# The front of a hybrid decoder block: every engine's order written out by hand instead of planned by priorities

## The chip, the cores and the metric

The kernel runs on one core of one Trainium2 chip. A core has TensorE (matrix products into PSUM), VectorE, ScalarE and GpSimd (called DVE, ACT and POOL in the profile) and SyncE, whose queue (SP) issues the DMA transfers here. Every engine works through its own queue in order and waits on semaphores for the others. The metric is device time in microseconds for one execution.

## What is computed

A decoder block over 512 positions of 1024 channels: a mixer of two halves (an S5 state space model and a chunked gating unit), then a PEER expert layer, then a gated embedding. The change concerns what stands ahead of PEER:

```python
xn = _rmsnorm(h, ln_mix_g[i])
z = xn @ w_in[i]
xs, u, v = z[..., :D_SSM], z[..., D_SSM:D_SSM + D_SGU], z[..., D_SSM + D_SGU:]
ys = _gelu(_s5(xs, ...))                               # diagonal complex recurrence + d * u
ys = ys * jax.nn.sigmoid(ys @ glu_w[i] + glu_b[i])
yg = _sgu(u, v, ...)                                   # gelu(u) * (tril(W_s) LN(gelu(v)) + b)
mix = jnp.concatenate([_rmsnorm(ys, out_norm_ssm[i]), _rmsnorm(yg, out_norm_sgu[i])], axis=-1)
h = h + mix @ w_out[i]
hn = _rmsnorm(h, ln_ffn_g[i])                          # PEER starts here
```

## The kernel before

Positions lie in four tiles of 128 (`NT`), channels in blocks of 128. The front goes through these stages, by the lines of `before.py`:

- x is loaded and transposed (L264), scaled into `xn` (L267, ScalarE), and multiplied with the first 512 columns of `w_in` in full f32 (`pz`, L278). ScalarE copies the product out by position modulo four into `u4` (L289), and VectorE scales it (L291).
- The embedding's projection `pj` (L304) has nothing to do with the rest; it is stored to memory (`pjd`) for the end of the kernel.
- VectorE works out the S5 parameters from 16-column tiles (L310 to L434): two exponentials, an angle, powers of the transition, squarings (`csquare`). From these come tables `rc`, `rs` of a complex exponential over 128 columns, doubled seven times (the `tab` loop under L557).
- The recurrence runs in four groups g of four pairs. `s5_r` makes operands on VectorE, `s5_par` (L481 to L498) transposes them on TensorE and copies them out on ScalarE, with a kernel matrix `ptt` whose third product adds the skip term d through an identity (L487); `s5_pv` (L506) makes the inputs of the scan, `s5_scan` (L518 to L526) scans on VectorE, `s5_back` rotates back, `s5_q` makes the output operands, `s5_out` (L543 to L548) multiplies them, and ScalarE applies sixteen Gelus into `ysT`.
- Two more f32 products with `w_in` give v and u (L601), followed by a Gelu (L604).
- `ysT` goes through the gated unit: `pg` (`glu_w`, split into a high and a low half so that three products replace an f32 one, `mm3`, L152 to L154), sigmoid (L629), product, `split_scaled`, square (L635). The squares are summed over channels by `prs` (L642).
- `w_out` has two halves: `wos` (products `po` with `mixs`, L659) and `w8` (with `mixg`, L715). Between them stand the normalisation of v (`norm_v`, L679 to L688) and its mixing (`mix_v`, L693 to L699).

In all of this the order of each engine's queue is not that of the source: a planner picks the next instruction by its priority, which `prio(...)` and the table `PR` shift. Only from the peer layer on is the order that of the source (`tc.manual_schedule()`, L729). Two PSUM pools, `psa` and `psb`, hold four banks each. Weights pass through `stage`, with `WB` = 6 buffers. `w_split` gives the low half of a split to VectorE or, in pieces of 256 columns, to GpSimd (L166).

Of the kernel before, what the change touches and what calls it, by code (L numbers as in the profile page):

```python
# [19 lines left out]
P = 128  # L20
# [31 lines left out]
PR = {"bc": -100, "glu": 100, "pj": 800, "po": -20, "q": -200, "r": -400, "s0": 50, "tab": 150, "uw": -100, "wglu": 100, "wog": 300, "wos": 150, "x": -20}  # L52
# [53 lines left out]
def tile_hybrid_block(ctx: ExitStack, tc: tile.TileContext, x, p_t, cols_d, rows_d, w_in, s5_b, s5_c, glu_w, ws_t,  # L106
# [29 lines left out]
    small = ctx.enter_context(tc.tile_pool(name="small", bufs=4))  # L136
    psums = ExitStack()
# [92 lines left out]
    with prio("m"):  # L230
        V.tensor_reduce(mt[:, :, 0:1], ident.rearrange("p (j t) -> p t j", t=L), axis=AX.X, op=ALU.add)
        V.tensor_copy(mt[:, :, 1:], mt[:, :, 0:1].to_broadcast([P, L, 31]))
        V.tensor_reduce(mj, ident.rearrange("p (j t) -> p j t", t=L), axis=AX.X, op=ALU.add)
    with prio("x"):
        for i in range(NT):
            S.activation(u4.rearrange("p a b -> p (a b)")[:, (i % 2) * D:(i % 2 + 1) * D], hsb[:, i, :], AF.Square,
                         accum_out=xr[:, i:i + 1])
        G.tensor_scalar(xr, xr, 1.0 / D, EPS, op0=ALU.mult, op1=ALU.add)
        G.tensor_tensor(xr, xr, mhalf[:, :NT], op=ALU.pow)
        G.tensor_tensor(xr4, mj[:, None, :].to_broadcast([P, NT, NJ // NT]), xr[:, :, None].to_broadcast([P, NT, NJ // NT]),  # L240
                        op=ALU.mult)

    def transpose_split(pool, tiles, gain, name):

        n = tiles[0].shape[-1] // P
        res = []
        for c in range(n):
            pt = pst("ptr")
            for i in range(NT):
                PE.transpose(pt[:, i * P:(i + 1) * P], tiles[i][:, c * P:(c + 1) * P], ident)  # L250
            hi, lo = (pool.tile([P, T], F32R, name=f"{name}{z}{c}") for z in "hl")
            split_scaled(hi, lo, pt, col(gain, c))
            res.append((hi, lo))
        return res
# [3 lines left out]
    with prio("warm"):  # L258
        for n in range(WARM):
            PE.transpose(pts[ND - 1][:, 0:P], ident, ident)  # L260
    with prio("xt"):
        for i in range(NT):
            for c in range(ND):
                PE.transpose(pts[c][:, i * P:(i + 1) * P], hsb[:, i, c * P:(c + 1) * P], ident)  # L264
    with prio("xn"):
        for c in range(ND):
            S.activation(xn[c], pts[c], AF.Copy, scale=col("ln_mix", c))  # L267


    with prio("z"):  # L270
        pz = [pst("pz", psa) for _ in range(NF)]
        for cc in range(ND // 2):
            with prio("zw" if cc else "zw0"):
                w2 = w_part(0, cc)
            for f in range(NF):
                for a, w in enumerate(w2):
                    c = 2 * cc + a
                    PE.matmul(pz[f], w[:, f * P:(f + 1) * P], xn[c], start=c == 0, stop=c == ND - 1)  # L278
    with prio("x4"):
        px = pst("px")[:, 0:P]  # L280
        PE.matmul(px, mt.rearrange("p t c -> p (t c)"), xr4.rearrange("p i j -> p (i j)"), start=True, stop=True)
        x4 = sp.tile([P, NJ], F32, name="x4")
        S.copy(x4, px)
    with prio("u4"):
        for f in range(NF):
            for q in range(4):
                for t in range(L):
                    e = S.copy if UEV[q] == "A" else V.tensor_copy
                    e(u4[32 * t:32 * t + 32, f * 4 + q, :], pz[f][32 * q:32 * q + 32, t:T:L])  # L289
            uf = u4[:, 4 * f:4 * f + 4, :]  # L290
            (V if U4S[f] == "V" else G).tensor_tensor(uf, uf, x4[:, None, :].to_broadcast([P, 4, NJ]), op=ALU.mult)  # L291


    pjd = dpool.tile([NT, P, D], F32, name="pjd")
    w_proj = gu_.rearrange("p (a b) n -> p a (b n)", a=2)
    nc.sync.dma_start(w_proj, ple_wp.rearrange("(a p) n -> p a n", p=P))
    for c in range(2):
        nc.sync.dma_start(ysT[c], p_t[c * P:(c + 1) * P, :])
    with prio("pj"):
        for i in range(NT):  # L300
            for o in range(2):
                pj = pst("pj")
                for c in range(2):
                    PE.matmul(pj, ysT[c][:, i * P:(i + 1) * P], w_proj[:, c, o * 512:(o + 1) * 512], start=c == 0, stop=c == 1)  # L304
                pjs = gv[(2 * i + o) % NT]
                S.copy(pjs, pj)
                nc.sync.dma_start(pjd[i, :, o * 512:(o + 1) * 512], pjs)


    with prio("s5p"):  # L310
        pq = [P, NPAIR]
        W = V
        cnt = [0]

        def pt16(name=None):
            cnt[0] += 1
            return sp.tile(pq, F32, name=name or f"s5p{cnt[0]}")

        def g_ts(o, i, s1, s2, op0, op1=None):
            if op1 is None:  # L320
                W.tensor_scalar(o, i, s1, None, op0=op0)
            else:
                W.tensor_scalar(o, i, s1, s2, op0=op0, op1=op1)

        def g_tt(o, a, b, op):
            W.tensor_tensor(o, a, b, op=op)

        LN2H, LN2L = 0.693359375, -2.12194440e-4

        def round_(o, i):  # L330
            g_ts(o, i, MAGIC, None, ALU.add)
            g_ts(o, o, MAGIC, None, ALU.subtract)

        def exp16(src, name):
            xx, n, r, q = (sp.tile(pq, F32, name=f"e{z}", tag=f"e{z}") for z in "xnrq")
            g_ts(xx, src, -87.0, 88.0, ALU.max, ALU.min)
            g_ts(n, xx, 1.0 / math.log(2.0), None, ALU.mult)
            round_(n, n)
            W.scalar_tensor_tensor(r, n, -LN2H, xx, op0=ALU.mult, op1=ALU.add)
            W.scalar_tensor_tensor(r, n, -LN2L, r, op0=ALU.mult, op1=ALU.add)  # L340
            g_ts(q, r, 1.0 / math.factorial(8), None, ALU.mult)
            for d in range(7, 0, -1):
                W.scalar_tensor_tensor(q, q, 1.0 / math.factorial(d), r, op0=ALU.add, op1=ALU.mult)
# [47 lines left out]
        for n in range(2, L + 1):  # L391
            cmul(W, pw[n][0], pw[n][1], *pw[n // 2], *pw[n - n // 2], t1)
# [911 lines left out]
```

## Time and profile before

| what | us |
|---|---|
| median of 3 runs (1594.93 to 1604.1) | 1602.31 |
| the profiled execution | 1601.3 |
| its span, first to last instruction | 1599.6 |
| TensorE busy over the span | 1536.4 |
| VectorE busy over the span | 1314.9 |
| first product of the peer layer (`pq`, L152) starts at | 246.1 |

The profile shows one execution. A line of its timeline has the start in us from the span's start, the length, engine, source line, operation, what it writes and reads, the shape and a count; in brackets stands how long the engine stood idle before it and what ended that. `x24` is a number of records: a full f32 product is two of them. TensorE's matmuls overlap, so the time that one costs is the distance between two starts, not its length.

### The profile page before, as it was taken

Reading aid. Unit: us, or ns where it says so; the run is one execution under the profiler, and the core shown is the slowest. Engines: PE = TensorE matmul, PEld = TensorE weight load, DVE = VectorE, ACT = ScalarE, POOL = GpSimd, SP = SyncE. Lnnn points to the kernel's source line nnn. Section 1 sums busy time; section 2 is a strip of 40 time slices with the busy share of each in tenths; the row PEclk is TensorE's granted clock in tenths of the full one; section 3 lists DMA queues with packets and bytes.
Section 4 is the critical chain, followed back from the end, with each engine's and each line's share of the span. In section 5 each row is a group of like instructions: output and inputs, shape, how many; then the busy total and the mean of one; then the engine's idle time right before and its main releaser. Section 6 shows DMA issues by size and latency. Waiting matters only on the chain.

```text
span 1599.6 us, 22230 instructions
## 1 busy us (share of the span) xinstructions
PE 1536.4 (96%) x7811; PEld 1337.2 (84%) x7811; DVE 1314.9 (82%) x2675; ACT 700.5 (44%) x1262; POOL 807.6 (50%) x680
## 2 busy tenths in 40 slices
PE   7998999999998998999999999999999999999998
PEld 4556687899998888888888888888888888888886
DVE  9885444799998777678899998988998999989774
ACT  3646424333336888843333333333333333333354
POOL 2012424458887878845455555545554555545201
PEclk9998899999999999999999999999999999999999
DMA  6111114223342454689898999989898989998851
GB/s 236 68 53 66 60 40 171 80 93 121 129 149 102 174 202 170 236 308 333 293 343 317 336 337 318 337 307 344 302 356 302 342 310 329 337 317 317 291 168 66
DMA packets 124432, 366.34 MB, mean 229 GB/s; under 512 B 8737, under 2 KB 60321, under 8 KB 106273
## 3 DMA queue, kind: packets, MB, share of 16 engines
q1 hardware_dynamic: 105888, 230.70, 42.1%
q0 software_dynamic: 18432, 134.23, 22.5%
q8 instruction: 61, 1.00, 0.2%
q14 instruction: 51, 0.41, 0.1%
HBM read 331.47 MB, written 33.42 MB: 228 GB/s over the span
## 4 chain that ended last, share of the span: by engine, by line
PE 62%; DVE 15%; ACT 7%; POOL 6%; issue 5%; DMA 4%; SPq 0%; POOLq 0%; ACTq 0%; DVEq 0%
PE yp L153 9%; PE yp L154 9%; PE yp L152 9%; PE pq L154 7%; PE pq L152 7%; PE pq L153 7%; ACT stg L1006 3%; DMA g<-in_uv,idx 3%; POOL ul L166 3%; PE pgm L1005 2%; PE pz L278 2%; DVE oh L878 1%; DVE oh L875 1%; PE pz L601 1%; PE pg L152 1%
## 5 line engine op out<-in xcount | busy, mean ns | idle before, releaser
L166 POOL TENSOR_TENSOR ul<-ust,uh 128x256 fp32r<-128x256 f32 (+1 forms) x342 | 430.3, 1284 | 187.2 <-ACT uh L159 186.9
L152 PE MATMUL pq<-hnh,uh 128*128 128x384 f32 (+1 forms) x1152 | 396.7, 344 | 0.8 <-DVE hnl L170 0.8
L154 PE MATMUL pq<-hnh,ul 128*128 128x384 f32 (+1 forms) x1152 | 394.9, 343 | 2.0 <-POOL ul L166 2.0
L153 PE MATMUL pq<-hnl,uh 128*128 128x384 f32 (+1 forms) x1152 | 393.5, 342 | 0.0
L1029 POOL DMA_INDIRECT g<-in_uv,idx x128 | 210.6, 1645 | 314.5 <-DVE y L1072 296.6
L153 PE MATMUL yp<-vl,ah 128*128 128x512 f32 x768 | 301.1, 392 | 4.5 <-DVE vl L161 4.5
L154 PE MATMUL yp<-vh,al 128*128 128x512 f32 x768 | 300.4, 391 | 0.0
L152 PE MATMUL yp<-vh,ah 128*128 128x512 f32 x768 | 298.9, 389 | 0.0
L793 ACT ACTIVATE gab<-pq 128x384 f32<-128x384 f32 x118 | 58.1, 492 | 483.8 <-PE pq L154 483.8
L152 PEld LDWEIGHTS pq<-hnh,uh 128*128 128x128 f32 x1152 | 217.3, 189 | 8.5 <-DVE hnl L170 1.0
L154 PEld LDWEIGHTS pq<-hnh,ul 128*128 128x128 f32 x1152 | 216.7, 188 | 9.0 <-POOL ul L166 3.3
L153 PEld LDWEIGHTS pq<-hnl,uh 128*128 128x128 f32 x1152 | 217.1, 188 | 7.8 <-DVE hnl L170 0.2
L161 DVE TENSOR_TENSOR vl<-vst,vh 128x1024 fp32r<-128x1024 f32 x128 | 161.9, 1265 | 22.1 <-ACT vh L159 21.9
L1061 DVE SCALAR_TENSOR_TENSOR g<-g,hrow 128x1024 f32<-128x1024 f32 x128 | 163.3, 1280 | 19.9 <-DMA g<-in_uv,idx 19.8
L153 PEld LDWEIGHTS yp<-vl,ah 128*128 128x128 f32 x768 | 144.1, 188 | 36.0 <-DVE vl L161 7.5
L154 PEld LDWEIGHTS yp<-vh,al 128*128 128x128 f32 x768 | 144.1, 188 | 29.9
L152 PEld LDWEIGHTS yp<-vh,ah 128*128 128x128 f32 x768 | 144.2, 188 | 28.4
L1072 DVE SCALAR_TENSOR_TENSOR y<-g,act,y 128x1024 f32<-128x1024 f32 x127 | 163.2, 1285 | 4.5
L1065 DVE TENSOR_TENSOR act<-act,gate 128x1 f32<-128x1 f32 (+1 forms) x117 | 156.6, 1339 | 0.0
L159 ACT CAST uh<-ust 128x1024 fp32r<-128x1024 f32 x144 | 150.8, 1047 | 0.0
L159 ACT CAST vh<-vst 128x1024 fp32r<-128x1024 f32 x128 | 134.2, 1049 | 2.3 <-DMA vst<-in_uv 2.2
L988 POOL TENSOR_SCALAR o1P<-iota,tr 128x128 f32<-128x128 f32 x96 | 110.9, 1165 | 3.6 <-ACT tr L945 3.6
(391 smaller groups left out, 2147.5 us busy)
## 6 DMA issues: line engine op xcount, KB each, us to landing
ust<-in_ut SPq DMA_DIRECT2D x128, 512.0 KB, 7.2
vst<-in_uv SPq DMA_DIRECT2D x128, 512.0 KB, 6.3
gd<-stg SPq DMA_DIRECT2D x12, 2048.0 KB, 7.2
gread<-gd SPq DMA_DIRECT2D x31, 768.0 KB, 8.4
ust<-in_wq SPq DMA_DIRECT2D x16, 512.0 KB, 3.5
wstage<-in_w_in SPq DMA_DIRECT2D x12, 512.0 KB, 5.7
wstage<-in_w_out SPq DMA_DIRECT2D x8, 512.0 KB, 3.9
ust<-in_ple_wg SPq DMA_DIRECT2D x8, 512.0 KB, 5.1
```

The lines of the kernel that those rows point to most:

```text
L152: PE.matmul(o, lh, rh, start=start, stop=False)
L153: PE.matmul(o, lh, rl, start=False, stop=False)
L154: PE.matmul(o, ll, rh, start=False, stop=stop)
L159: S.copy(hi, src)
L161: V.tensor_tensor(lo, src, hi.bitcast(F32), op=ALU.subtract)
L166: G.tensor_tensor(l[:, sl], s[:, sl], h[:, sl], op=ALU.subtract)
L793: S.activation(ga[n], p_[:, 0:TD], AF.Gelu)
L988: (V if e == "V" else G).tensor_scalar(o1[a], iota, i1, g, op0=ALU.is_equal, op1=ALU.mult)
L1029: G.indirect_dma_start(out=gt, out_offset=None, in_=uv, in_offset=bass.IndirectOffsetOnAxis(ap=idx[:, r:r + 1], axis=0))
L1061: V.scalar_tensor_tensor(GS[k][:, 0:D], GS[k][:, 0:D], 1.0, hrow0, op0=ALU.mult, op1=ALU.mult, accum_out=dots[:, k:k + 1])
L1065: V.tensor_tensor(act[:, k:k + n], act[:, k:k + n], gates[0][:, k:k + n], op=ALU.mult)
L1072: V.scalar_tensor_tensor(y0, t[:, D:], act[:, k:k + 1], y0, op0=ALU.mult, op1=ALU.add)
```

## The change

From the first loads up to the peer layer every engine now takes its instructions in the order of the source, which is written out anew (`tc.manual_schedule()` moves to the top; `prio` is used no more). The order mixes the groups of the S5 part with a `filler`: the `pj` products and the v and u products, doled out one `next` at a time. `fill(2)` is one `pj` product (two matmuls), later `fill(1)` is one v or u matmul. Three things are done otherwise, too. Every low half of a weight split is made on VectorE. The skip term is added by VectorE in PSUM in a new function `s5_par2`, which also has the copies into `t4`; its product is gone. The `rhos` copy stands behind the z products instead of ahead of `xn`. The additions of `ln_b` go from GpSimd to VectorE, the temporaries of table and scan share one buffer, and `pj` takes its PSUM banks from `psa`.

```diff
     small = ctx.enter_context(tc.tile_pool(name="small", bufs=4))
+    ctx.enter_context(tc.manual_schedule())
...
+    loads = [("z", cc) for cc in range(ND // 2)] + [("v", cc) for cc in range(ND // 2)] + [("g", 0), ("g", 2)] \
+        + [("u", cc) for cc in range(ND // 2)] + [("o", c) for c in range(2 * NF)]
+    def load(n=NW):
+        while loads and n and (len(ORD) - len(loads) < WB or ORD[len(ORD) - len(loads) - WB] not in WT):
...
     def s5_par(g):
...
-            PE.matmul(o, flat(ri[:, q]), nci[:, 4 * g + q, :], start=False, stop=False)
-            PE.matmul(o, ident, skip[:, 4 * g + q, :], start=False, stop=True)
+            PE.matmul(o, flat(ri[:, q]), nci[:, 4 * g + q, :], start=False, stop=True)
...
+    def s5_par2(g):
+        t4, ptt = TT[g]
         k3 = ptt[:, 0:P].rearrange("p (q c) -> p q c", q=4)
+        k0 = k3[(L - 1) * 32:]
+        V.tensor_tensor(k0, k0, skip[(L - 1) * 32:, 4 * g:4 * g + 4, :], op=ALU.add)
         S.copy(t4[:, :, 3, :], k3)
         for t in range(3):
             for b in range(t + 1):
                 S.copy(t4[32 * b:32 * b + 32, :, t, :], k3[32 * (b + 3 - t):32 * (b + 4 - t)])
...
+    def table_steps():
+        sq = csquare(csquare((e1c, e1s)))
+        n = 1
+        while n < NJ:
...
+                V.tensor_tensor(o, a, b, op=op)
+                if 2 * n == NJ:
+                    yield
             n *= 2
+            if n in (16, 64):
+                yield
+            if n < NJ:
+                sq = csquare(sq)
...
+    def filler():
+        for k in range(2 * NT):
+            i, o = divmod(k, 2)
+            pj = pst("pj", psa)
...
+            S.copy(pjs, pj)
+            nc.sync.dma_start(pjd[i, :, o * 512:(o + 1) * 512], pjs)
+            yield
+            yield
+        for kind, dst in (("v", gv), ("u", gu)):
+            ph = [pst("pz", psa) for _ in range(NT)]
+            for cc in range(ND // 2):
+                w = WT.pop((kind, cc))
                 for i in range(NT):
+                    for a in range(2):
...
+                        if c == ND - 1:
+                            S.activation(dst[i], ph[i], AF.Gelu, scale=xr[:, i:i + 1])
+                        yield
+                load()
...
+    z_mm(0)
+    s5_r(0, V)
+    z_mm(1)
...
+    S.copy(x4, px)
+    S.copy(rhos, rho[:, :, None].to_broadcast([P, NPAIR, NJ]))
+    G.memset(rhos[:, :, 0:1], 0.0)
+    s5_r(1, V)
+    s5_par(0)
+    z_mm(2)
+    s5_par(1)
+    tab = table_steps()
+    next(tab)
+    s5_par2(0)
+    next(tab)
+    s5_par2(1)
+    z_mm(3)
+    u4_copy(0)
+    for n in range(4):
+        next(tab)
+    u4_scale(0)
+    for n in range(3):
+        next(tab, None)
+    fill(2)
+    s5_pv(0)
+    u4_copy(1)
+    fill(2)
+    s5_r(2, V)
+    u4_scale(1)
+    s5_scan(0)
+    s5_pv(1)
+    u4_copy(2)
+    fill(2)
+    s5_par(2)
+    s5_par2(2)
+    u4_scale(2)
+    s5_scan(1)
+    u4_copy(3)
+    fill(4)
+    s5_pv(2)
+    s5_back(0, "V")
+    u4_scale(3)
+    s5_q(0)
+    fill(13)
+    s5_r(3, V)
+    s5_out(0)
+    w_glu = []
+    for c in (0, 2):
+        w_glu += w_split(WT.pop(("g", c)), fp, f"wglu{c}", V)
+        load()
+    s5_scan(2)
+    fill(8)
+    s5_par(3)
+    s5_pv(3)
+    s5_back(1, "V")
+    s5_par2(3)
+    s5_q(1)
+    fill(6)
+    s5_scan(3)
+    s5_out(1)
+    s5_back(2, "V")
+    s5_q(2)
+    fill(14)
+    s5_back(3, "V")
+    s5_out(2)
+    s5_q(3)
+    fill(6)
+    nv = [norm_v(0)]
+    s5_out(3)
...
+    fill(12)
+    for f in range(3):
+        ys_split(f)
+    norm_v2(0, *nv[0])
+    nv.append(norm_v(1))
+    ys_split(3)
+    wo_split(0)
+    wo_split(1)
+    norm_v2(1, *nv[1])
+    nv.append(norm_v(2))
+    pgs = [glu_mm(fo) for fo in range(NF)]
+    fill(8)
+    for fo in range(2):
+        glu_mix(fo, pgs[fo])
+    norm_v2(2, *nv[2])
+    nv.append(norm_v(3))
+    for fo in range(2, NF):
+        glu_mix(fo, pgs[fo])
+    fill(100)
...
+    wo_split(2)
+    norm_v2(3, *nv[3])
+    wo_split(3)
+    prs = pst("prs")
     for i in range(NT):
+        for f in range(NF):
+            PE.matmul(prs[:, 2 * i:2 * i + 2], ysT[f][:, i * P:(i + 1) * P], ones, start=f == 0, stop=f == NF - 1)
...
+    pms = [mix_v(i) for i in range(NT - 1)]
+    for c in range(NF, 2 * NF):
+        wo_split(c)
+    grs = [mix_v2(i, pms[i]) for i in range(NT - 1)]
...
+    po_s(0, 0)
...
+    for k in range(1, 6):
+        po_s(*divmod(k, 2))
...
+    for k in range(6, 8):
+        po_s(*divmod(k, 2))
+    for i in range(NT):
+        po_g(i)
```

`z_mm(cc)` is a fourth of the z products; `u4_copy` and `u4_scale` are L289 and L291 for one block; `ys_split` and `wo_split` split a block of `ysT` and of `w_out` (ScalarE casts the high half, VectorE subtracts); `norm_v` makes the statistics of L679 to L683 and `norm_v2` applies them; `glu_mix` has sigmoid, product, the two halves and the square of one block, in this order; `mix_v` and `mix_v2` are L693 and L696 to L699; `po_s` and `po_g` are the products and additions of L659 and L715.

More of the change, by code (lines that the diff above doesn't have):

```diff
@@ L243, in transpose_split @@
[L243 to L254, printed above, removed]
+    V.tensor_reduce(mt[:, :, 0:1], ident.rearrange("p (j t) -> p t j", t=L), axis=AX.X, op=ALU.add)
@@ L270, in tile_hybrid_block @@
[L270 to L307, printed above, removed]
@@ L438, in tile_hybrid_block @@
[L438 to L445 removed]
+    for i in range(NT):
+        for c in range(ND):
+            PE.transpose(pts[c][:, i * P:(i + 1) * P], hsb[:, i, c * P:(c + 1) * P], ident)
@@ L564, in tile_hybrid_block @@
-            bc = lambda a: a[:, :, None].to_broadcast([P, NPAIR, n])
-            cmul(V, rc[:, :, n:2 * n], rs[:, :, n:2 * n], rc[:, :, 0:n], rs[:, :, 0:n], bc(en[0]), bc(en[1]), tt[:, :, 0:n])
-            n *= 2
-    with prio("pv"):
-        s5_pv(0)
-    with prio("scan"):
-        s5_scan(0)
-    for g in range(1, NF):
-        with prio("r"):
-            s5_r(g, V if RENG[g] == "V" else G)
-        with prio("q"):
-            s5_q(g)
-        with prio("par"):
-            s5_par(g)
-        with prio("pv"):
-            s5_pv(g)
-        with prio("scan"):
-            s5_scan(g)
-        with prio("back"):
-            s5_back(g - 1, BACK[g - 1])
-        with prio("out"):
-            s5_out(g - 1)
@@ L586, in tile_hybrid_block @@
-    with prio("back"):
-        s5_back(NF - 1, BACK[NF - 1])
-    with prio("out"):
-        s5_out(NF - 1)
-    for off, dst in ((1024, gv), (512, gu)):
-        pz = [pst("pz", psa) for _ in range(NT)]
-        for cc in range(ND // 2):
-            with prio("uw" if off == 512 else "vw"):
-                w2 = w_part(off, cc)
-            with prio("u" if off == 512 else "v"):
+            tt = fw.tile([P, 3 * 4 * NJ], F32, name="tt", tag="sc", bufs=1)[:, 0:NPAIR * NJ // 2].rearrange(
+                "p (a j) -> p a j", a=NPAIR)
@@ L636, in tile_hybrid_block @@
-    with prio("wos"):
-        wo = [w_split(w_load(w_out[c * P:(c + 1) * P, :], 1, D), rp_, f"wos{c}", G if c % 2 else V)[0] for c in range(NF)]
-    with prio("prs"):
-        prs = pst("prs")
-        for i in range(NT):
-            for f in range(NF):
-                PE.matmul(prs[:, 2 * i:2 * i + 2], ysT[f][:, i * P:(i + 1) * P], ones, start=f == 0, stop=f == NF - 1)
-        rss = small.tile([P, 2 * NT], F32, name="rss")
-        V.tensor_copy(rss, prs[:, 0:2 * NT])
-        rss = rstd_of(rss, 2 * NT, 1.0 / DS)
@@ L675, in norm_v, with fill @@
+                        if c == ND - 1:
+                            S.activation(dst[i], ph[i], AF.Gelu, scale=xr[:, i:i + 1])
+                        yield
+                load()
+    fill_ = filler()
+    def fill(n):
+        for _ in range(n):
+            next(fill_, None)
     def norm_v(i):
@@ new lines, in tile_hybrid_block, with ys_split @@
+    s5_q(1)
[11 more added lines that the diff above has]
+    s5_out(3)
+    assert not PV and not HH
+    s5.close()
+    late = ExitStack()
+    rp_ = late.enter_context(tc.tile_pool(name="late", bufs=1, side="right"))
+    ysp = []
+    def ys_split(f):
+        hi, lo = (rp_.tile([P, T], F32R, name=f"ys{z}{f}") for z in "hl")
+        split_sb(hi, lo, ysT[f])
+        ysp.append((hi, lo))
```

480 lines of the change are left out of this document (245 added, 235 removed).

## The prediction

> **What bounds the kernel now.** I read the page first, then the busy time by stretch, then the chain that ended last.
>
> ```profile
> span 1599.6 us, 22230 instructions
> PE 62%; DVE 15%; ACT 7%; POOL 6%; issue 5%; DMA 4%; SPq 0%; POOLq 0%; ACTq 0%; DVEq 0%
> ```
>
> TensorE carries most of the chain. The change touches only what comes before the peer layer, whose last product feeds the VectorE addition at 239.76 us; behind it the source is the same, so only that point moves.
>
> ```profile
> 11.00:61.10 50.10, 43.99 (x98) 18.89 (x99) 44.83 (x201) 27.05 (x81) 4.70 (x10) 0.97 0.45 162
> 61.10:144.20 83.10, 77.30 (x380) 53.30 (x379) 64.02 (x143) 35.50 (x91) 6.80 (x16) 0.94 0.13 42
> 144.20:181.30 37.10, 33.43 (x119) 21.28 (x117) 13.88 (x15) 30.45 (x48) 11.07 (x12) 0.93 0.35 120
> 181.30:240.40 59.10, 54.09 (x241) 44.11 (x241) 29.72 (x51) 11.76 (x28) 25.27 (x41) 0.93 0.08 28
> ```
>
> The columns are the stretch, its length, busy time of TensorE, its weight loads, VectorE, ScalarE and GpSimd, then granted clock and DMA. In all four stretches TensorE is busy about nine tenths; VectorE is nearly as full in the first two, and lighter later. What holds TensorE up in the later ones is in the chain:
>
> ```profile
> 144.13 1.04 ACT wos0h L159
> ...
> 167.78 9.44 PE pz L601 x22
> ...
> 189.35 3.17 POOL w8l L166 x4
> ...
> 239.76 0.70 DVE hsb L715
> ```
>
> ScalarE's casts stand ahead of its last Gelus, and a GpSimd weight split holds `wsm` and `pm` back. A better order could win something: TensorE rows below price its work.
>
> ```profile
> 14.69 29.43 PE L278 MATMUL pz<-xn,wstage 128*128 128x512 f32 x64 [3.79 <-ACT xn L267]
> ...
> 96.02 0.39 PE L544 MATMUL py<-hs,qr 128*128 128x128 f32 x2
> 96.24 0.39 PE L545 MATMUL py<-hs,qi 128*128 128x128 f32 x2
> ...
> 98.47 11.32 PE L601 MATMUL pz<-wstage,xn 128*128 128x512 f32 x26
> ...
> 143.81 7.03 PE L601 MATMUL pz<-wstage,xn 128*128 128x512 f32 x16
> ...
> 165.58 0.39 PE L152 MATMUL pg<-ysh,wglu0h 128*128 128x512 f32 x1
> 165.81 0.39 PE L153 MATMUL pg<-ysl,wglu0h 128*128 128x512 f32 x1
> ...
> 181.85 0.63 PE L153 MATMUL po<-wos0l,mixh 128*128 128x512 f32 x1
> 182.28 0.63 PE L154 MATMUL po<-wos0h,mixl 128*128 128x512 f32 x1
> ...
> 192.83 1.66 PE L693 MATMUL pm<-gv,wsm 128*128 128x128 f32 x8 [3.80 <-POOL wsm L672]
> ```
>
> A full f32 product is two records of 0.43, so 0.87 us; a small record costs 0.11 (0.22 for two); a split product 0.23, and 0.43 at the half clock of 181.85. The front needs 112 f32 products (97 us), 240 split ones (54) and, once the skip products are gone, some 350 small records (39): 190 us. Begun at 11, that would end at 201 against 239.7. So there are nearly 39 us to win at most; the question is how many the fixed order leaves waiting.
>
> **The change, part by part.** Four edits are cheap. The skip product (32 records of 0.11, 3.6 us of TensorE) becomes four VectorE additions on 32 partitions; no such row exists, between a 16-element (0.17) and a 512-element operation (0.68) I take 0.25. The GpSimd splits move to VectorE, five of 1024 elements. The additions of ln_b move too, four of 512. Together some 9 us of VectorE, whose cover in the later stretches is its load of a half or less; where VectorE sets the pace, 2 splits and 4 skip additions (3.3 us) stand in its chain and are in the sums below. And `rhos` no longer stands ahead of `xn`:
>
> ```profile
> 12.15 1.90 ACT L444 COPY rhos<-rho 128x2048 f32<-128x2048 f32 x1 [1.75 <-DVE rho L326]
> ...
> 39.01 9.38 ACT L289 COPY u<-pz 32x128 f32<-32x128 f32 x35 [20.32 <-PE pz L278]
> ...
> 147.09 6.45 ACT L548 ACTIVATE ysT<-py 32x128 f32<-32x128 f32 x16
> ...
> 158.60 1.28 ACT L629 ACT_TABLE_LOAD   x1
> ...
> 167.82 0.69 ACT L629 ACTIVATE sg<-pg,cols 128x512 f32<-128x512 f32 x1 [0.32 <-PE pg L154]
> ...
> 170.81 0.63 ACT L635 ACTIVATE ysT<-ysT 128x512 f32<-128x512 f32 x1 [0.82 <-DVE mixl L170]
> ...
> 177.26 3.88 ACT L159 CAST w8h<-wstage 128x1024 fp32r<-128x1024 f32 x4 [1.03 <-PE pz L601]
> ```
>
> With `xn` from 10.5, z starts at about 11.2 instead of 14.7 and misses the half-clock stretch behind that pause: 5 us ahead, and all four z steps could end at 39.
>
> The dear edit is the order. A scheduler interleaves independent chains on VectorE; the written order emits each chain whole:
>
> ```profile
> 5.22 1.22 DVE L343 SCALAR_TENSOR_TENSOR eq<-eq,er 128x16 f32<-128x16 f32 x6
> ...
> 8.16 0.17 DVE L321 TENSOR_SCALAR s5p<-s5p 128x16 f32<-128x16 f32 x1
> 8.24 0.17 DVE L340 SCALAR_TENSOR_TENSOR er<-en,er 128x16 f32<-128x16 f32 x1
> ...
> 46.19 1.22 DVE L187 TENSOR_TENSOR rc<-rc,s5p 128x1024 f32<-128x1024 f32 x1
> ...
> 134.02 1.22 DVE L526 TENSOR_TENSOR_SCAN sg<-rhos,sc 128x512 f32<-128x512 f32 x1
> ...
> 138.19 0.68 DVE L190 TENSOR_TENSOR hs<-rc,sg 128x512 f32<-128x512 f32 x1
> 138.79 0.68 DVE L188 TENSOR_TENSOR hs<-hs,tm 128x512 f32<-128x512 f32 x1
> 139.51 0.69 DVE L189 TENSOR_TENSOR tm<-rs,sg 128x512 f32<-128x512 f32 x1
> ```
>
> Behind an independent operation the next starts 0.08 before its end; behind one that it depends on, or whose operand it overwrites (L189 behind L188), 0.04 after it. For 16 elements that is 0.08 against 0.21. `cmul` written out has three such pairs in six operations. So by estimate, from these rows and the next two: the parameter chain has 105 operations, about 80 of them held, 20 us; an `s5_r` 4.9; `s5_back` and `s5_q` 4.0 each; a scan 6.1; the table 11 to its sixteenth column, 9 more to its 64th, 1.3 for a squaring and 7.2 for the last level.
>
> ```profile
> L187 DVE TENSOR_TENSOR rrr<-prr,rrr 128x384 f32<-128x384 f32 x4 | 2.2, 552 | 0.0
> L187 DVE TENSOR_TENSOR rrr<-s5p,b_pad 128x128 f32<-128x128 f32 x4 | 1.1, 286 | 1.2 <-PE pw L492 1.2
> L679 DVE BATCH_NORM_STATS2 bnst<-gv 128x6 f32<-128x128 f32 x16 | 4.0, 265 | 0.0
> L680 DVE BATCH_NORM_AGGREGATE bnmv<-bnst 128x2 f32<-128x6 f32 x16 | 2.4, 166 | 0.0
> ```
>
> The DMA queue loses nothing. Its loads now stand in the order of use, each behind the release of a buffer six loads earlier, so `pjd`'s stores wait behind the `glu_w` loads for the fourth z step; nobody reads them before the end. The last three `w_out` loads follow the last u product at 179, and land some 4 us later:
>
> ```profile
> wstage<-in_w_out SPq DMA_DIRECT2D x8, 512.0 KB, 3.9
> ```
>
> Their casts come at 195 or later. GpSimd's mask of `wsm` moves to the start and waits there for its load, with only the `t4` clearing behind it, which is not needed before 43.
>
> Now the walk, first the S5 part. VectorE: parameters to 22.5, two `s5_r` to 32.3, table to the 64th column with the first skip addition at 52.4. The second skip addition comes only then. In ScalarE's queue the seven `t4` copies that wait for it (1.9 us by the 0.27 of row 39.01) stand ahead of `u4_copy(0)` (16 of 0.27), though its `pz` has been done since 42; that copy ends at 58.9. TensorE has z and two `s5_par` (24 records, 2.7 each) done at 46.8; the next thing in its queue, the first `pj`, now takes a bank of the pool that `pz` still holds. So it waits 12 us, with `s5_pv(0)` and the v products queued behind it, then runs some 4 us at half clock; `s5_pv(0)`, which also needs `u4_scale(0)` behind four operations of the table's last level, ends at 65.
>
> From there VectorE sets the pace: `s5_r(2)`, scan 0, scan 1, back 0, q 0 and `s5_r(3)` end at 94.5, TensorE's `s5_out(0)` at the same time. Next on VectorE are the low halves of `w_glu`, whose ScalarE casts stand behind sixteen Gelus (6.5): VectorE idles to 102. Scan 2, held behind them, keeps two PSUM banks that `s5_par(3)` needs (TensorE waits some 6). Then back 1, q 1 (118.8, TensorE's `s5_out(1)` waits 3.6), scan 3, back 2, q 2, and back 3, which needs `s5_out(2)` finished for its single buffer (136.3), then q 3: `s5_out(3)` ends at 147.1 with 41 of the 64 u and v products done. Before, TensorE was through with it at 143.8 (row 143.81) and had 16 and 22 records left, 19 products, so 45 done.
>
> Then the gated unit. Twelve u products to 157.5, `pg` with a wait of 1.3 for the fourth `ysl` to 169.7 (48 of 0.23), eight u products to 176.6. ScalarE's queue holds the Gelus of `gu` 0 and 1 ahead of the first sigmoid, so `glu_mix` starts at 177.8 behind a table load (1.28). Each `glu_mix` goes from ScalarE to VectorE and back twice: 3.6 us from sigmoid to the end of the square, by the rows at 167.82 and 170.81, and the next sigmoid stands behind that square. Between the second and third VectorE also has `norm_v2(2)` (2.6: four of 0.28 and two held of 0.7) and `norm_v(3)` (1.6, a quarter of L679 and L680): four mixes end at 194.9. TensorE has its last u product at 179.2, and `prs` is next in its queue and needs the fourth square: a wait of 15.7 us. What stands behind it waits too: `pm`, all 16 `po`, the transposes. After such a pause the clock is half, as at 192.83 (eight records in 1.3): `prs` 6, `pm` 5.3, to 206.4. From there all is fed, VectorE's last six splits included: 16 `po` of 2.73 and 1.8 of transposes end at 251.9.
>
> Sum: 251.9 − 239.7 = +12 us. The profiled execution took 1601.3 (span 1599.6 and 1.7 around it), so 1613.5; the median of the runs shown is 1602.3, so 1614. Between bounds: no half clock at `prs` takes 5 off; a bank for `s5_par(3)` that is free earlier takes up to 4 off, unless VectorE is late anyway; waits that I have not seen add.
>
> **The rivals.** (a) Faster: TensorE is not held at `prs`. The place is the queue between the last u product and `prs`, the price 15.7 of waiting and 5.5 of half clock: 1614 − 21 = 1593. It decides from the point where the four mixes fit in front of 179; overlapped as at 163 to 171 us of the trace they cost 2.5 each, and then still 6 is missing, unless the sigmoids run ahead of the Gelus. The written order on ScalarE speaks against it; VectorE's load of a third there speaks for it.
>
> (b) Within 0.5%: chained operations cost no more than free ones (0.08 for small, duration less 0.08 for large). The parameters then end at 12.5, `s5_r(1)` at 24.6, the table's 64th column at 39, so ScalarE copies u as pz ends, `s5_out(0)` ends at 79.5 and `s5_out(3)` at 130: 17 us less, 1597. The rows at 5.22 and 139.51 speak against it. [...] The trace disagrees: 0.21 against 0.08.
>
> (c) Slower still: one more wait of ten, where a load sits behind a waiting one in the SP queue or a PSUM bank is chosen badly: 1624.
>
> (d) The written order is not what the queues hold, and little changes: 1602.
>
> **How the numbers follow.** Forecast 0.52, a 0.15, b 0.18, c 0.10, d 0.05. A measurement of this kernel can tell about 0.5% (8 us) from no change. The forecast's own spread, 1606 to 1621, puts 0.05 of it within 0.5%. Faster is rival a and a little of b: 0.18; within, the rest of b, d and that 0.05: 0.25; slower 0.57. The range from 1592 to 1625 leaves out part of a and of c.
>
> **What would show it.** In the changed profile: z from about 11; a TensorE wait of some 12 before the first `pj`, released by the `u` copies; VectorE waiting 7 for the cast of `wglu`; `s5_out(3)` at 147; and a wait of 15 of `prs` for `ysT`, with half clock behind it. A last `po` before 235 would prove me wrong, above all if `prs` follows the u products without a pause.

## The result, and the profile after

| what | before | after |
|---|---|---|
| median of four runs, us | 1601.6 (1594.9 to 1604.1) | 1621.6 (1619.0 to 1624.4) |
| ratio, 95% interval | | 1.0132 [1.0096, 1.0167] |
| span of the profiled execution | 1599.6 | 1618.7 |
| last `po` addition starts | 239.76 | 254.46 |
| first product of the peer layer (`pq`) starts | 246.11 | 267.56 |

The kernel became slower by 20 us. In the timeline of the profiled execution it is 14.7 late at the last `po` addition and 21.4 late at the first `pq`. The second number is the measure used below. It is finer than a time: the same instructions keep the distance of 21.4 in the two profiles up to 497 us (of the kernel before), then it wanders to 18.1 by 680 and is 19.1 at the span's end, and the times of the kernel before, over all its runs, lie between 1594.9 and 1606.6: a single time can be 5 to 7 us off.

First the timeline of TensorE after the change, the rows behind the idle times that the argument needs: start, length, line, operation, count; in brackets the idle time and what ended it.

```profile
11.43 14.00 PE L523 MATMUL pz<-xn,wstage 128*128 128x512 f32 x32 [0.71 <-ACT xn L272]
61.59 3.78 PE L564 MATMUL pj<-gu,ysT 128*128 128x512 f32 x4 [12.52 <-ACT u L530]
146.50 0.49 PE L512 MATMUL py<-hs,qi 128*128 128x128 f32 x2 [1.56 <-DVE qi L435]
183.57 0.38 PE L767 MATMUL prs<-ones,ysT 128*128 128x2 f32 x2 [2.26 <-ACT ysT L714]
187.07 0.58 PE L767 MATMUL prs<-ones,ysT 128*128 128x2 f32 x2 [3.12 <-ACT ysT L714]
193.28 0.58 PE L767 MATMUL prs<-ones,ysT 128*128 128x2 f32 x2 [5.62 <-ACT ysT L714]
196.78 5.71 PE L767 MATMUL prs<-ones,ysT 128*128 128x2 f32 x26 [2.92 <-ACT ysT L714]
```

The z products start 3.3 earlier than before, as the missing `rhos` copy allows, and lose it again: 12.5 at the first `pj`, and at `prs` four waits that add up to 13.9, one for each square. VectorE's timeline has the other two places of the walk, the second skip addition and the splits of `w_glu`:

```profile
54.95 0.32 DVE L460 TENSOR_TENSOR ptt<-ptt,skip 32x128 f32<-32x128 f32 x1
105.09 1.23 DVE L162 TENSOR_TENSOR wglu0l<-wstage,wglu0h 128x1024 fp32r<-128x1024 f32 x1 [7.28 <-ACT wglu0h L160]
```

Busy time by stretch, first of the kernel after, then of the kernel before in the same stretches (columns as in the prediction):

```profile
11.00:62.00 51.00, 35.64 (x115) 19.46 (x116) 46.76 (x203) 16.48 (x44) 8.30 (x20) 0.88 0.41 150
178.00:209.00 31.00, 17.08 (x76) 14.52 (x75) 18.19 (x35) 17.91 (x23) 5.14 (x4) 0.67 0.06 18
209.00:255.20 46.20, 45.42 (x206) 36.98 (x204) 20.62 (x41) 10.40 (x26) 7.22 (x18) 1.00 0.11 35
255.20:267.60 12.40, 6.18 (x33) 5.39 (x33) 5.72 (x7) 3.23 (x6) 4.71 (x7) 0.72 0.96 336
```

```profile
11.00:62.00 51.00, 44.89 (x107) 19.75 (x107) 45.73 (x203) 27.64 (x82) 4.70 (x10) 0.97 0.47 166
178.00:209.00 31.00, 27.20 (x123) 22.89 (x123) 14.81 (x27) 5.90 (x11) 17.43 (x24) 0.83 0.09 26
```

TensorE (the first busy column) loses 9 us in the first stretch and 10 around `prs`, and in both its granted clock is lower too (0.88 against 0.97, 0.67 against 0.83). From 209 it is full; then, behind the last addition, half empty for 12 us. That last stretch is not in the prediction. The chain that ended last shows it, after and then before (start, length, engine, tile, line):

```profile
254.46 0.70 DVE hsb L787
...
255.25 0.73 ACT junk L788 x2
...
256.14 0.27 POOL rstd L791
...
257.00 0.25 POOL iota L835
...
257.27 0.81 DVE number L843
258.08 1.13 DVE hrow L904
259.21 1.13 DVE hrowuh L904
260.35 1.14 DVE hrowul L904
...
261.54 4.47 PE ptr L912 x23
```

```profile
239.76 0.70 DVE hsb L715
...
241.32 0.33 PE ptr L823
...
241.74 2.83 PE ptr L823 x24
```

From the last addition to the first `pq` it is 13.1 after and 6.35 before. In the kernel before, three of the four scalings of `hrow` (L815) ran between the additions of `po` (L715), each as soon as its row was complete, and the copy `number` ran at 216.94. Both stand in the source behind L729, from where on the order is the source's, but they ran among the additions from ahead of it all the same: only among themselves do the instructions behind L729 keep the source's order. VectorE's timeline of the kernel before has them:

```profile
226.00 0.75 DVE L815 TENSOR_SCALAR hrow<-hsb,rstd 128x1024 f32<-128x1024 f32 x1 [1.87 <-POOL rstd L720]
...
231.44 0.75 DVE L815 TENSOR_SCALAR hrowuh<-hsb,rstd 128x1024 f32<-128x1024 f32 x1 [1.86 <-POOL rstd L720]
...
236.93 1.22 DVE L815 TENSOR_SCALAR hrowul<-hsb,rstd 128x1024 f32<-128x1024 f32 x1 [1.93 <-POOL rstd L720]
```

With the planner gone they run where the source has them, behind the last addition, and `number` with its `iota` ahead of them: 4.2 us. TensorE then starts its transposes after a longer pause and runs most of them at half pace (4.47 instead of 2.83, at a granted clock of 0.50 from 261.5 to 264.0, where it was 1.00 before): 1.6 more. The remaining 0.9 are small waits, the one for `iota` among them.

### The profile page after: what moved, and what is told of

Same layout as the page of the kernel before. It is cut to its first block, busy times and chain, and to the rows that moved or that the text cites. A ratio compares the mean times of both kernels' runs of the same rounds, so it can differ in the third digit from the quotient of the medians.

```text
span 1618.7 us, 22140 instructions
## 1 busy us (share of the span) xinstructions
PE 1533.8 (95%) x7779; PEld 1334.0 (82%) x7779; DVE 1337.1 (83%) x2688; ACT 700.5 (43%) x1262; POOL 788.9 (49%) x656
## 4 chain that ended last, share of the span: by engine, by line
PE 60%; DVE 18%; ACT 7%; POOL 5%; issue 5%; DMA 4%; SPq 0%; POOLq 0%; DVEq 0%; ACTq 0%
PE yp L154 9%; PE yp L155 8%; PE yp L153 8%; PE pq L155 7%; PE pq L153 7%; PE pq L154 7%; ACT stg L1095 3%; DMA g<-in_uv,idx 3%; POOL ul L167 3%; PE pgm L1094 2%; PE pz L577 1%; DVE oh L967 1%; DVE oh L964 1%; POOL g L1118 1%; PE pg L154 1%
## 5 line engine op out<-in xcount | busy, mean ns | idle before, releaser
L162 DVE TENSOR_TENSOR vl<-vst,vh 128x1024 fp32r<-128x1024 f32 x128 | 161.9, 1265 | 21.9 <-ACT vh L160 21.7
L153 PEld LDWEIGHTS yp<-vh,ah 128*128 128x128 f32 x768 | 144.2, 188 | 28.4
```

The costliest lines, as they stand in the source:

```text
L153: PE.matmul(o, lh, rh, start=start, stop=False)
L162: V.tensor_tensor(lo, src, hi.bitcast(F32), op=ALU.subtract)
```

## The experiments

All kernels derive from the changed kernel, except run e11. "`out(3)`" is the end of the last `s5_out` product, "`po`" the start of the last addition, "`pq`" how much later than before the first `pq` starts; these three are read from one profiled execution of each run. Each ratio is taken against executions of the kernel before in the same batch, whose medians lie between 1600.7 and 1602.6.

| run | `out(3)` | `po` | `pq` | time, us (runs) | ratio to before, 95% |
|---|---|---|---|---|---|
| before | 144.0 | 239.8 | 0 | 1601.6 (4) | |
| after | 149.0 | 254.5 | +21.4 | 1621.6 (4) | 1.0132 [1.0096, 1.0167] |
| e1_tail | 150.6 | 256.0 | +15.2 | 1616.5 (1) | |
| e2_glu | 149.4 | 241.2 | +8.1 | 1611.8 (4) | 1.0064 [1.0047, 1.0081] |
| e3_par2 | 148.9 | 254.9 | +22.2 | 1624.8 (1) | |
| e4_wglu | 141.8 | 247.0 | +13.8 | 1616.7 (1) | |
| e5_three | 141.8 | 231.9 | −8.1 | 1595.4 (4) | 0.9953 [0.9937, 0.9970] |
| e6_spaced | 145.6 | 250.8 | +17.7 | 1618.7 (1) | |
| e7_skip_product | 149.6 | 254.2 | +21.9 | 1626.0 (1) | |
| e8_gpsimd_splits | 147.9 | 253.3 | +20.3 | 1625.2 (1) | |
| e9_five | 141.0 | 235.8 | −5.0 | 1599.8 (10) | 0.9986 [0.9969, 1.0003] |
| e10_six | 141.1 | 233.2 | −7.6 | 1596.6 (8) | 0.9969 [0.9952, 0.9985] |
| e11_before_parts | 144.2 | 229.8 | −11.0 | 1597.6 (7) | 0.9969 [0.9950, 0.9988] |
| e12_spaced_overlap | 137.9 | 227.2 | −12.9 | 1590.3 (6) | 0.9929 [0.9903, 0.9954] |

The landmark `pq` is not the time, for the stretch behind it varies. In e9 the first `pq` is 5.0 early and the median 1.1 below that of the kernel before in its batch; in e11 it is 11.0 and 3.2. The last column decides what a kernel is worth, and the landmarks show where it comes from.

### e1_tail: the scalings back between the additions

```diff
-    for i in range(NT):
+    for i in range(NT - 1):
         po_g(i)
+    last = [out_mm(mixg, NF, NT - 1, o) for o in range(2)]
...
+    for i in range(NT - 1):
+        V.tensor_scalar(hrow[i], hsb[:, i, :], hr_[i], None, op0=ALU.mult)
+    po_g(NT - 1, last)
```

> The changed kernel, with the scalings of hrow 0 to 2 and their buffers ahead of the last two po additions, and the number copy behind the last scaling. Theory: behind the last addition (254.46 in the changed kernel) stand 0.2 of waiting and 0.73 of the number copy and three scalings of 1.13 that the planner had put between the additions; taken out, the first hn transpose starts some 4.4 us earlier, about 2 us behind the last addition (before: 1.6), and the time is 1617. Rival: the transposes wait for something else that is late (the gab row's load, which landed at 259.17, or GpSimd), and the distance stays at 5 or more: 1620 to 1621.

The chain that ended last, in this run:

```profile
256.00 0.70 DVE hsb L787
...
256.78 0.73 ACT junk L788 x2
...
257.56 1.87 PE ptr L916 x15
```

The first transpose on the chain stands 1.6 behind the last addition, as before, and the transposes run at the pace of the kernel before again (15 in 1.87, there 24 in 2.83). From addition to `pq` it is now 5.3 (261.33 for the `pq`) instead of 13.1: the tail's 6.75 and one more are back. The rival, something else that is late there, is out: nothing on this chain waits for a load or for GpSimd. The `po` column is 1.5 later than in the changed kernel although the edit changes nothing ahead of the last additions; what that is stands in the last section.

### e2_glu: the sigmoids ahead of the last u products' Gelus, the norms of v 2 and 3 behind them

```diff
-    pgs = [glu_mm(fo) for fo in range(NF)]
-    fill(8)
-    for fo in range(2):
-        glu_mix(fo, pgs[fo])
+    for fo in range(NF):
+        glu_mix(fo, glu_mm(fo))
     norm_v2(2, *nv[2])
...
```

> The changed kernel, with each glu_mix right behind its pg products, the last u products, their Gelus and the norms of v 2 and 3 behind all four. Theory: prs waited 13.9 for the fourth square only because ScalarE held the sigmoids behind the gu Gelus. Now the squares are done by about 178, the u products cover them, prs follows without a pause of over 2 us, and the granted clock behind it stays near 1.0: the last po addition moves from 254.5 to some 236 (18 less), the time to 1603. Rival: VectorE's norms and the casts of w_out become the wait that takes its place (pm needs norm_v2(3), po needs wo2 and wo3), and half of it comes back: 1612. Rival of the prediction (its a) would be right in mechanism if the gain is over 15.

TensorE's timeline of this run:

```profile
181.58 0.73 PE L763 MATMUL prs<-ones,ysT 128*128 128x2 f32 x6
182.82 3.06 PE L763 MATMUL prs<-ones,ysT 128*128 128x2 f32 x26 [0.51 <-ACT ysT L714]
185.74 4.51 PE L719 MATMUL pm<-gv,wsm 128*128 128x128 f32 x24
192.43 1.16 PE L719 MATMUL pm<-gv,wsm 128*128 128x128 f32 x8 [2.18 <-DVE rss L765]
```

The waits of `prs` shrink from 13.9 to 0.5 and its 26 records run in 3.1 instead of 5.7. The edit changes two queues, and ScalarE's timeline tells their parts apart. The first square starts at 171.62 instead of 182.89, the second at 175.12 instead of 186.39: 11.3 earlier, because the sigmoids no longer stand behind two Gelus of `gu`. The third and fourth are 14.0 earlier: the other 2.7 are the two norms that VectorE had between the second and third block. So ScalarE's queue was the larger cause and VectorE's the smaller. The last addition comes 13.3 earlier, not 18. The rival has part of the rest: `pm` waits 2.2 for `rss`, which VectorE reads out behind a norm and two splits. The time, 1611.8, is the one that the rival named, not the theory's 1603.

### e3_par2: the second skip addition behind `u4_copy(0)`

```diff
-    s5_par2(1)
     z_mm(3)
     u4_copy(0)
+    s5_par2(1)
```

> The changed kernel, with the second skip addition and its seven t4 copies behind u4_copy(0). Theory: the first pj starts some 9 to 11 us earlier (from 61.6 to about 51), but VectorE sets the pace, so out(0) (from 97.4) and out(3) move by at most 2 us and the time by 0 to 2: 1619 to 1621. Rival: TensorE's 12 us pause is what the front pays for; then the last po addition moves by 8 or more: 1612.

```profile
52.63 1.99 PE L564 MATMUL pj<-gu,ysT 128*128 128x512 f32 x4 [2.84 <-ACT u L530]
62.97 2.07 PE L472 MATMUL pv<-u,w4r 128*128 128x128 f32 x8 [8.36 <-DVE u L534]
```

In TensorE's timeline `pj` starts 9 earlier, and 8.4 of it are waited off one step on, at the first `pv`, for VectorE's `u4_scale`. `out(3)` and `po` stay within 0.5. The largest single wait of the front costs nothing by itself, since VectorE sets the pace there.

### e4_wglu: the casts of `w_glu` ahead of the sixteen Gelus

```diff
-    s5_out(0)
     w_glu = []
...
+    s5_out(0)
```

> The changed kernel, with both w_glu splits ahead of s5_out(0), so that their casts stand ahead of the sixteen Gelus on ScalarE. Theory: VectorE loses its wait of 7.3 and scan 2 starts at about 100 instead of 107.4; out(3) ends some 5 us earlier, not 7, since TensorE then has its v products still to do ahead of out(1) and out(2); the last po addition moves by about 5: 1616. Rival: TensorE is as full as VectorE here and the gain is under 2: 1620.

VectorE splits `w_glu` at 97.9 instead of 105.1 with no wait in front. `out(3)` and the last addition come 7.2 and 7.5 earlier. The theory had 5 and allowed TensorE a part; it took none. Here a wait of 7.3 on VectorE's path was worth its whole length.

### e5_three: e1, e2 and e4 together

> The changed kernel with the three edits of the runs tail, glu and wglu together. Theory: they are three waits in a row on one path (VectorE's at 98 to 105, TensorE's at 183 to 197, VectorE's behind the last addition), so their gains add: against the kernel before, the first product of the peer layer with keys was 21.5 later in the changed kernel; 7.7, 13.3 and 7.5 come off, so it stands about 7 earlier than before, and the time is 1595. Rival: TensorE is the bound once two of them are gone, and the third gives nothing: level with before, 1602.

The first `pq` starts 29.6 earlier than in the changed kernel; the three gains one by one add up to 6.2 + 13.4 + 7.6 = 27.2. The waits stood in a row. The kernel is now faster than the one before by 0.5%, with every other part of the change in it.

### e6_spaced: no operation behind the one it needs

```diff
-    def cmul(e, o_re, o_im, ar, ai, br, bi, t1):
+    def cmul(e, o_re, o_im, ar, ai, br, bi, t1, t2=None):
+        if t2 is not None:
+            e.tensor_tensor(t1, ai, bi, op=ALU.mult)
+            e.tensor_tensor(o_re, ar, br, op=ALU.mult)
+            e.tensor_tensor(t2, ai, br, op=ALU.mult)
+            e.tensor_tensor(o_im, ar, bi, op=ALU.mult)
+            e.tensor_tensor(o_re, o_re, t1, op=ALU.subtract)
+            e.tensor_tensor(o_im, o_im, t2, op=ALU.add)
+            return
...
```

> The changed kernel, with the operations of a complex product, of the scans 0 and 1 and of q 0 in an order in which no operation follows the one it depends on (a second temporary; up to s5_out(0) only). Theory: a chained operation costs 0.12 to 0.13 more than a free one; some 65 of them go by the end of s5_r(3), which moves from 97.8 to about 89.5; the first pj, which waits for the second skip addition, from 61.6 to 56.5, and since TensorE is full from there, out(0) and the last po addition move by about 5: 1616. Rival (b of the prediction): chained operations cost nothing extra, nothing moves: 1621.

The last complex product of `s5_r(3)` on VectorE, first in the changed kernel, then here:

```profile
94.54 0.56 DVE L187 TENSOR_TENSOR t<-pri,rri 128x384 f32<-128x384 f32 x1
95.01 0.55 DVE L188 TENSOR_TENSOR rrr<-prr,rrr 128x384 f32<-128x384 f32 x1
95.60 0.56 DVE L189 TENSOR_TENSOR rrr<-rrr,t 128x384 f32<-128x384 f32 x1
...
97.25 0.56 DVE L192 TENSOR_TENSOR rri<-rri,t 128x384 f32<-128x384 f32 x1
```

```profile
89.11 0.56 DVE L188 TENSOR_TENSOR t<-pri,rri 128x384 f32<-128x384 f32 x1
89.58 0.55 DVE L189 TENSOR_TENSOR rrr<-prr,rrr 128x384 f32<-128x384 f32 x1
90.05 0.55 DVE L190 TENSOR_TENSOR tz<-pri,rrr 128x384 f32<-128x384 f32 x1
...
91.45 0.56 DVE L193 TENSOR_TENSOR rri<-rri,tz 128x384 f32<-128x384 f32 x1
```

The same six operations take 2.34 from first to last start instead of 2.71: 0.12 for each of the three pairs. The chain to the end of `s5_r(3)` is 5.8 shorter, not 8.3. The first `pj` moves to 56.8, as expected; the last addition moves by 3.7, not 5, and VectorE now waits 9.6 for the cast of `w_glu` instead of 7.3.

### e7_skip_product and e8_gpsimd_splits: the other two parts undone

```diff
-            PE.matmul(o, flat(ri[:, q]), nci[:, 4 * g + q, :], start=False, stop=True)
+            PE.matmul(o, flat(ri[:, q]), nci[:, 4 * g + q, :], start=False, stop=False)
+            PE.matmul(o, ident, skip[:, 4 * g + q, :], start=False, stop=True)
```

> The changed kernel, with the skip term back in TensorE's third product and no addition in PSUM. Theory: the addition costs little by itself; its price is the queue behind it. Without it the t4 copies need not wait for VectorE, the first pj starts at about 51 instead of 61.6, but VectorE sets the pace and has only 4 times 0.35 less: the last po addition moves by 0 to 2, earlier, 1620. Rival: TensorE's 32 extra products (3.6 us) tell, and it is 2 to 4 later.

```diff
-        w_glu += w_split(WT.pop(("g", c)), fp, f"wglu{c}", V)
+        w_glu += w_split(WT.pop(("g", c)), fp, f"wglu{c}", G if c else V)
...
-        wo[c] = w_split(WT.pop(("o", c)), rp_, f"wo{c}", V)[0]
+        wo[c] = w_split(WT.pop(("o", c)), rp_, f"wo{c}", G if c % 2 else V)[0]
```

> The changed kernel, with the low halves of wglu2 and of every odd block of w_out back on GpSimd. Theory: the splits on VectorE have cover but for wglu2, whose 1.14 stands ahead of scan 2: the last po addition moves by about 1, earlier: 1620. Rival: GpSimd's split of 3.2 us holds a po product back (wo3 is needed for the first one at 208), and it is 2 to 4 later: that would be what the edit brings.

The last addition moves by 0.3 and 1.2, both earlier, and both less than the 1.6 by which two traces of the same queues differed (last section). (In e7 the first `pj` comes to 56.3, not to 51; as in e3 it makes no difference.) Neither part makes the changed kernel slow. Their single times lie 4.3 and 3.6 above its median, and e3's 3.1, with a first `pq` within 1.2 of its: in these traces the stretch behind the first `pq` is 3.6 to 5.6 longer, though nothing was changed there.

### e11_before_parts: these two parts in the planner's order

Here the kernel before gets `s5_par`'s addition in PSUM and `V` for every weight split; the order stays the planner's.

> The kernel before, order by the planner, with the two other parts of the change alone: the skip term added on VectorE in PSUM and every low half of a weight split on VectorE. Theory: the order is the whole loss; these two parts lose nothing and win what the runs on the changed kernel say (about 0.3 and 1.2), perhaps the 3.8 that pm waited for GpSimd: 1598 to 1602. Rival: the additions and splits stand in VectorE's way and cost: 1606 or more.

TensorE's timeline at the place where the kernel before waited 3.80 for GpSimd's mask (row 192.83 of the prediction):

```profile
186.29 1.16 PE L694 MATMUL pm<-gv,wsm 128*128 128x128 f32 x8 [0.46 <-POOL gv L689]
```

`pm` starts 6.5 earlier, the first `pq` 11.0 in the profiled execution; the median falls by 0.3%, and its interval ends below 1. So with these two parts the planner's kernel gains. That the whole gain is theirs isn't shown, since the planner may also have ordered other instructions anew around them. All of the loss, 32.5 us from this kernel's first `pq` (235.09) to that of the changed kernel, belongs to the order and the small moves that came with it.

### e9_five and e10_six: more products moved ahead

Run e9 is e5 with e6's spacing, the second skip addition behind the first four `pj` products, and `fill(8)` ahead of the first `pv`.

> The run with three edits, and two more: the spaced order of the run before last, and eight TensorE matmuls of pj (and later eight v matmuls) ahead of the first pv, with the second skip addition behind them. Theory: VectorE has 34 of 35.6 us busy from 62 to 97.6 and 19.0 of 19.4 from there to 117, so it sets the pace; some 8 us of its chain go, and TensorE, fed in its pause at 50 to 62, can follow: out(0) to out(3) and the last po addition some 6 earlier than in the run with three edits (231.9), about 226: 1589. Rival: TensorE is the bound there by now, and only 1 or 2 come: 1594.

Neither range came true. `out(3)` came 0.7 earlier and the last addition 3.9 later than in e5. TensorE's timeline:

```profile
159.21 0.50 PE L154 MATMUL pg<-ysl,wglu2h 128*128 128x512 f32 x1 [3.50 <-DVE ysl L162]
175.37 0.59 PE L791 MATMUL prs<-ones,ysT 128*128 128x2 f32 x2 [3.12 <-ACT ysT L742]
178.87 5.70 PE L791 MATMUL prs<-ones,ysT 128*128 128x2 f32 x26 [2.92 <-ACT ysT L742]
```

and ScalarE's, just before:

```profile
147.94 0.69 ACT L607 ACTIVATE gu<-pz,xr 128x512 f32<-128x512 f32 x1 [0.46 <-PE pz L605]
...
151.96 2.17 ACT L160 CAST ysh<-ysT 128x512 fp32r<-128x512 f32 x4
```

With nine more of the filler's matmuls done by `s5_out(0)`, all but two of the u products end ahead of `pg`, and three of their four Gelus, written at the last product of each block, slide in front of the casts of `ysT`: the first low half of `ysT` comes at 152.6, in e5 at 148.9. And two u products are too few to cover the squares, so `prs` waits again, and again runs at half pace (5.70, at a granted clock of 0.50 from 174 to 186). The wait is back where e2 had removed it.

Run e10 adds to e9 that the four `glu_mix` chains overlap, with the norms of v in VectorE's gaps:

```diff
+    for fo in range(NF):
+        glu_mix(fo, sgs[fo])
+        if fo < 3:
+            sgs.append(glu_sig(fo + 1, pgs[fo + 1]))
+        if fo % 2:
+            nv.append(norm_v(2 + fo // 2))
+        else:
+            norm_v2(1 + fo // 2, *nv[1 + fo // 2])
+        glu_mix2(fo)
```

> The run of five edits, and the four glu_mix chains overlapped: the next sigmoid ahead of the last square, the norms of v 1 to 3 in the gaps of VectorE, no norm ahead of the first product. Theory: in the run with three edits VectorE stood idle for 7 of 18 us there, and the first product waited 5.4 behind norms; the squares come 3 to 4 earlier, VectorE reaches the pm stage with its norms done, and the last po addition is 4 earlier than in the run of five: 1585. Rival: the u products (or their end) hold prs anyway: 0 to 1, 1589.

The last addition came 2.6 earlier than in e9, not 4; still later than in e5.

### e12_spaced_overlap: e5, e6 and the overlap, fills left alone

> The run with three edits, with the spaced order and the overlapped glu_mix chains, but the fills of pj, v and u where the changed kernel has them: eleven u products are left behind pg. Theory: what went wrong in the runs of five and of six was that products moved ahead left TensorE without cover at pg and prs; with the cover back, the spaced order gives the 3.7 that it gave alone and the overlap the 2.6 that it gave from five to six: the last po addition at about 226 instead of 231.9, 1589. Rival: the first pj starts at 56.5 and TensorE is the bound from there, so that only one of the two counts: 229 to 231, 1593 to 1595.

Between 140 us and the last addition TensorE's timeline of this run names only two idle times, and none at `prs`:

```profile
151.68 0.50 PE L154 MATMUL pg<-ysl,wglu2h 128*128 128x512 f32 x1 [1.12 <-DVE ysl L162]
178.39 1.52 PE L754 MATMUL pm<-gv,wsm 128*128 128x128 f32 x8 [1.84 <-DVE rss L805]
```

The last addition at 227.2 and the time of 1590.3 lie nearer to the theory's 226 and 1589 than to the rival's 229 and 1593; the addition came 4.7 earlier than in e5, where the two edits alone had given 3.7 and 2.6. This kernel has the lowest median of all: it is 0.7% faster than before, and its first `pq` starts 34.3 earlier than that of the changed kernel, with the same products and the same two other parts. Only the order differs, and the second temporary.

## Why the prediction was right, and where it fell short

The forecast was 1614, slower by 12, by waits that the written order makes. It came out slower by 20 (1621.6), inside the range, and the waits are where the walk put them:

- z from 11.2: 11.43. TensorE waits 12 at the first `pj`: 12.5, granted clock 0.88 in the stretch to 62 and 0.50 from there to 65. It also said that VectorE sets the pace from there, and e3 shows that the wait costs nothing while that holds.
- VectorE waits 7.6 for the cast of `w_glu`: 7.3, and e4 shows that it costs 7.5 at the end.
- `out(3)` ends at 147.1: 149.0. VectorE's chain was walked too short: the second skip addition comes at 54.95, where the walk had the table and both additions at 52.4.
- The four mixes end at 194.9: the last `prs` row starts at 196.78. `prs` waits 15.7: 13.9. `prs` and `pm` at half clock, 11.3 together: 11.4 from 196.78 to the first `po` at 208.2, at a granted clock of 0.50 up to 202.5 and 0.60 behind it. (The row at 192.83, on which the forecast put its half clock, has 0.72 over its eight records.)
- The end of the last `po`: +12 forecast, +14.7 measured. Of the 2.5 more, 1.9 are there already at `out(3)`.
- Two waits of TensorE were walked too long: some 6 at `s5_par(3)` and 3.6 at `s5_out(1)`. The first is 0.7 there and 2.1 one step on, at `s5_pv(3)`, the second 1.6. VectorE is busy for 27.96 of the 28.6 from 107.4 to 136, so it carried the end.

The step that failed is the sentence on which the sum ended: "behind it the source is the same, so only that point moves". The source is the same there, but three scalings and a copy did not run where it has them: **in the kernel before they had run ahead of that point**. The term had been sized at nothing and measures 6.75 us; e1 takes it back. With 2.5 us from the walk it makes the 9 us by which the first `pq` is later than the sum said, and 2.3 of those are lost again in the drift behind.

Rival a (TensorE not held at `prs`) was right about its place and too dear: removing the wait in e2 is worth 13.3, not 21, because VectorE's norms and splits and a granted clock of 0.84 from 182 to 194 take its place. It put the deciding point at sigmoids ahead of the Gelus, and that is the larger part of the edit that worked.

Rival b (chained operations are free) is refuted by e6: the six operations take 2.34 instead of 2.71, 0.12 less for each pair that is no longer chained, and the chain moved by 5.8 and the last addition by 3.7.

Rival c (one more wait of ten, behind a load or a badly chosen PSUM bank, 1624) is nearer to the measured 1621.6 than the forecast is, but not by its mechanism: what the forecast lacked stands behind the last addition in VectorE's queue, and e1 takes it back by moving VectorE's instructions.

Rival d (the order is not what the queues hold) has nothing left: in every stretch shown here the queues of the changed kernel hold the source's order.

The prediction priced the skip addition and the splits on VectorE as edits with cover. In the written order they cost 0.3 and 1.2 (e7, e8). What it did not see is that the planner's kernel wins with the two together (e11); how much of that is the splits' alone wasn't tried: it named the GpSimd wait ahead of `pm` and worked out no gain from it.

## What to carry to other kernels

When a planner's order is replaced by the source's, walk the whole queue of each engine to the next point where all engines meet, not to the end of the edited text: instructions that the planner had pulled ahead fall back to where they are written. In these runs a wait on the engine that set the pace was worth its full length (7.3 of VectorE's gave 7.5 in e4), and waits in a row added up (6.2, 13.4 and 7.6 one by one, 29.6 together in e5); one on another engine was worth nothing (e3, where the first `pj`, which had waited 12.5, came 9 earlier and the last addition did not). Work moved ahead to fill a pause takes its followers along in every other queue (e9, where the last addition came 3.9 later than in e5), so keep enough of it behind to cover the next pause.

## What the runs showed of the hardware

**Behind the same pause TensorE's half pace fell differently in two traces.** In e1_tail and in the changed kernel the queues are the same up to the tail and the first `pj` starts at 61.62 and 61.59; the stretch behind it, first of the changed kernel, then of e1_tail:

```profile
61.60:75.00 13.40, 12.20 (x49) 7.86 (x49) 12.34 (x23) 9.17 (x34) 0.59 (x3) 0.79 0.10 39
```

```profile
61.60:75.00 13.40, 11.27 (x42) 7.22 (x43) 12.41 (x24) 9.18 (x34) 0.59 (x3) 0.75 0.10 39
```

The granted clock is 0.79 and 0.75, TensorE is seven records behind, and everything from there to the last addition is 1.5 to 1.7 later in e1_tail. In the changed kernel the clock is 0.50 from 61.6 to 65.0, and the eight `pv` records at 65.17 still take 1.70 from their first start to the next row's; in e1_tail the eight at 65.17 take 0.89. Behind the next wait (1.20 in the changed kernel, 2.10 in e1_tail) it is the other way round: eight `pv` records take 0.90 from 71.97 in the changed kernel and 1.68 from 71.94 in e1_tail, the four `pj` records behind them 1.71 and 2.60. From the start of the first `pj` to that of the `rri` transposes of `s5_par(2)` it is 16.1 in the changed kernel, 16.0 in e5 and 17.7 in e1_tail: one trace of these three. So a landmark behind this pause was off by 1.6 us. Behind two pauses of the changed kernel the records themselves took longer: the transposes of the tail 1.6 (4.47 at a granted clock of 0.50 up to 264.0, against 2.83 at 1.00 in the kernel before), the 26 records of `prs` 2.6 (5.71 at 0.50, against 3.06 in e2 at 0.84 from 182 to 194).

**VectorE's scalings took 1.21 to 1.22 beside a GpSimd split and 0.74 to 0.75 without one.** With GpSimd idle when it starts, a scaling of `hrow` takes 0.75 (226.00 and 231.44 in the kernel before). `hrowul` at 236.93 there takes 1.22, and so do all three behind the last addition in the changed kernel (1.21 each, 1.13 from start to start). GpSimd's timelines, of the kernel before and of the changed kernel, have a split of the peer layer's first weights at those moments (in the changed kernel it ends at 260.93, and the fourth scaling, at 261.40, takes 0.74):

```profile
236.87 3.27 POOL L166 TENSOR_TENSOR ul<-ust,uh 128x256 fp32r<-128x256 f32 x4
```

```profile
257.22 3.71 POOL L167 TENSOR_TENSOR ul<-ust,uh 128x256 fp32r<-128x256 f32 x4
```

The copy `number` takes 0.28 at 216.94 before, with GpSimd idle, and 0.81 at 257.27 after, beside the split. So by estimate from these rows (three times 0.46 and once 0.53) some 1.9 of the 4.2 us in the tail are length that these four had only beside the split. That the split caused it is not shown: no run moved it alone.
